# Three SSD products moved from GpSimd to VectorE, and one running account for the background work of a tick

## The chip, the cores and the metric

The kernel runs on one core of one Trainium2 chip. The metric is the device time of one execution in microseconds (us); lower is better. TensorE is called PE below, VectorE DVE, ScalarE ACT, GpSimd POOL, and SyncE, which issues the transfers, SP.

## The reference

One step of a one-layer hybrid decoder: 2048 prompt tokens and 8 sample sequences of 4 tokens share the weights. A wide projection feeds a convolution branch (value times sigmoid of a gate, a depthwise convolution of 31 taps) and a Mamba-2 branch, which are merged and projected.

```python
proj = h @ w_in
conv_val, conv_glu, conv_gate, z, xbc, dt_raw, m_conv, m_ssm = split_cols(proj, IN_SIZES)
u, new_conf_buf = causal_dwconv(conv_val * jax.nn.sigmoid(conv_glu), conf_buf, conf_dw_w, conf_dw_b)
...
xbc = jax.nn.silu(xbc)
xs, bm, cm = split_cols(xbc, ...)
# ssd_scan, in chunks of 128 tokens
decay = jnp.exp(jnp.where(mask, seg, -jnp.inf))
cb = jnp.einsum('bcqgn,bckgn->bcqkg', cc, bc)
y_intra = jnp.einsum('bcqkgr,bckgrp->bcqgrp', cb[..., None] * decay, xdt)
st = jnp.einsum('bcqgn,bcqgrp->bcgrpn', bc, xdt * decay_end[..., None])
y_inter = jnp.einsum('bcqgn,bcgrpn->bcqgrp', cc, h_starts) * jnp.exp(cum)[..., None]
...
y = y.reshape(bsz, L, SSM_DIM) * jax.nn.silu(z)
y = rmsnorm(y.reshape(bsz, L, SSM_GROUPS, SSM_DIM // SSM_GROUPS), 1.0).reshape(bsz, L, SSM_DIM) * ssm_norm_g
```

## The kernel before

There are two passes. Pass 1 (to about 2460 us) does the wide projection with the SSD scan inside it; pass 2 does the output projections. The change touches pass 1 alone.

**Ticks.** Pass 1 treats the tokens in two halves: half 0 has 1056 tokens in three token blocks of 352 columns, half 1 has 1024 in two blocks of 512. Within a half it goes through eight groups of heads; a group has ten blocks of weights (B, C, four of x, a merge block, the gates and values of the convolution, an even and an odd z). One block of weights times one token block is a tick: 24 matmuls in `mm3`, since each fp32 product is made of a high and a low part (`hh`, `hl` and `wh`, `wl`; L136 to L138). The result lies in a PSUM tile `acc` until `evac` reads it. The low part of each weight tile is made on DVE at L129, the high part on ACT at L128.

**SSD units.** A unit is one chunk of 128 tokens for one group of four heads. Half 0 has nine units in a group, half 1 eight, and a new one begins every three or two ticks. `prefetch` loads a tile `se` of 128x1024 from memory; ACT subtracts and clips it (L611, four times) and takes the exponential (L613). Its first half then holds factors by which C is scaled, its second half (`un["m"]`) the decay matrix. `ssd_a_pe` makes transposes and the product C times B on PE; `ssd_a_vec` makes out of them `cbm` (L654), the scaled x `xe` and `xd` (L661, L662), the high parts `bt` and `xh` on ACT, and the low parts `bl` (L671, DVE) and `xl` (L669, POOL). The scaling of C (L652) and the product of decay and `cbm` (L656) are on POOL, too. Some ticks later (four in half 0, three in half 1, two in group 7) `ssd_b_pe` uses all of it: PE L701 reads the product, L704 the scaled C, L710 to L712 the parts of x and B. `ssd_b_vec` adds up on DVE (L723 to L733).

**Gating.** After a z block ACT makes its silu (L775), DVE multiplies it onto the group's output (`set`, L806). After the odd block ACT squares (L813), DVE adds the two squares (`sp`, L814) and PE sums over the group (L825, `group_sums`), in the program two ticks later (`SUMS_AGE`); ACT takes that sum out of PSUM at L828. PE works in program order: where L814 is late, PE stands still at L825.

**Background work.** Three queues of generators fill DVE between these: `hi` (the four-tap convolution of x, B and C, L543), `mid`, and `lo` (the 30 taps of the other convolution, L574, each 128x1024). In each tick a budget is set (3300 in half 0, 5000 in half 1), the unit's costs are taken off (1450 and 1700), `hi` runs with what is left, and `lo` with what `hi` leaves, but with no less than 1200. Each tick starts with a new budget. A scheduler then orders the instructions of each engine by their priorities (`PRIO_*`); what it decides is shown below for the places at issue.

Of the kernel before, what the change touches and what calls it, by code (L numbers as in the profile page):

```python
# [7 lines left out]
F32 = mybir.dt.float32  # L8
# [17 lines left out]

PRIO_SPLIT, PRIO_EVAC, PRIO_MID, PRIO_SSD = 300, 300, 100, 100
GATE_AT = 5
SUMS_AGE = 2
T2 = 416  # L30
NT2 = NTOK // T2
# [9 lines left out]
for _n, _w in (("sw", 128), ("sb", 32), ("cw", 248), ("cb", 8), ("lng", 8), ("lnb", 8), ("dsk", 16),  # L41
               ("ng", 16), ("gpre", 8), ("gpost", 8), ("bada", 24), ("alog", 32), ("dtb", 1)):
    PRM[_n] = (_o, _w)
    _o += _w
NPRM = _o

CST = {}
_o = 0
# [37 lines left out]
class Kernel:  # L86
# [560 lines left out]
    def ssd_a_vec(self, un):  # L647
        V, S = self.V, self.S
        half, g, c, se, tr, w = (un[k] for k in ("half", "g", "c", "se", "tr", "w"))
        hs = slice(4 * g, 4 * g + 4)  # L650
        if c < 8 and not un["zero"]:
            self.G.tensor_tensor(out=se[:, 0:4], in0=se[:, 0:4], in1=bc(un["C"], "p (o q) -> p o q", [P, 4, P], o=1), op=ALU.mult)  # L652
        cbm = self.a1.tile([P, P], F32, tag="cbm", name="cbm", bufs=2)
        V.tensor_tensor(out=cbm[:w, :w], in0=tr[:w, 384:384 + w], in1=self.c_("tri") if c < 8 else self.c_("btri", NH)[:, :NH], op=ALU.mult)  # L654
        M = un["m"][:w, :, :w]
        self.G.tensor_tensor(out=M, in0=M, in1=bc(cbm[:w, :w], "p (o q) -> p o q", [w, 4, w], o=1), op=ALU.mult)  # L656
        xd = self.a1.tile([P, 4, 64], F32, tag="xd", name="xd", bufs=2)
        xe = self.a1.tile([P, 4, 64], F32, tag="xe", name="xe", bufs=1)
        w3 = w if c < 8 else 96
        xt = tr[:w3, 0:256].rearrange("p (h q) -> p h q", h=4)  # L660
        V.tensor_tensor(out=xe[:w3], in0=xt, in1=bc(self.dte[half][:w3, c, hs], "p (h o) -> p h o", [w3, 4, 64], o=1), op=ALU.mult)  # L661
        V.tensor_tensor(out=xd[:w], in0=xt[:w], in1=bc(self.dt[half][:w, c, hs], "p (h o) -> p h o", [w, 4, 64], o=1), op=ALU.mult)  # L662
        bt = self.a1.tile([P, P], F32R, tag="bt", name="bt", bufs=2)
        if c < 8:
            S.activation(out=bt, in_=tr[:, 256:384], func=AF.Copy)
            xh = un["xh"] = self.a1.tile([P, 4, 64], F32R, tag="xh", name="xh", bufs=2)
            S.activation(out=xh, in_=xe, func=AF.Copy)  # L667
            xl = un["xl"] = self.a1.tile([P, 4, 64], F32R, tag="xl", name="xl", bufs=2)
            self.G.tensor_tensor(out=xl, in0=xe, in1=xh.bitcast(F32), op=ALU.subtract)  # L669
            bl = un["bl"] = self.a1.tile([P, P], F32R, tag="bl", name="bl", bufs=2)  # L670
            V.tensor_tensor(out=bl, in0=tr[:, 256:384], in1=bt.bitcast(F32), op=ALU.subtract)  # L671
        else:
            S.activation(out=bt[:96], in_=tr[:96, 256:384], func=AF.Copy)
            V.tensor_tensor(out=bt[64:96], in0=tr[64:96, 256:384], in1=bt[64:96].bitcast(F32), op=ALU.subtract)
            xr = un["xr"] = self.a1.tile([P, 4, 64], F32R, tag="xr", name="xr")
            S.activation(out=xr[:96], in_=xe[:96], func=AF.Copy)
            V.tensor_tensor(out=xr[32:64], in0=xe[32:64], in1=xr[32:64].bitcast(F32), op=ALU.subtract)
            bm = self.se_tile().rearrange("p a q -> p (a q)").bitcast(F32R).rearrange("p (s n) -> p s n", s=NS)
            V.tensor_tensor(out=bm[:96], in0=bc(bt[:96].bitcast(F32), "p (o n) -> p o n", [96, NS, P], o=1),
                            in1=bc(self.c_("smask", 96), "p (s o) -> p s o", [96, NS, P], o=1), op=ALU.mult)  # L680
            un["bm"] = bm
        un["bt"], un["cbm"], un["xd"], un["xe"] = bt, cbm, xd, xe
# [74 lines left out]
    def evac(self, half, blk, tb, acc, env):  # L757
# [12 lines left out]
        elif kind in ("z", "gate", "m"):  # L770
            t = self.spp.tile([P, TB], F32, tag="sp", name="sp")
            if kind == "m":
                S.activation(out=t[:, :w], in_=acc[:, :w], func=AF.Tanh, scale=0.5)
            else:
                S.activation(out=t[:, :w], in_=acc[:, :w], func=AF.Silu)  # L775
            if kind == "z":
                self.gating(half, blk[1], off, w, t)
            else:
                Q.dma_start(self.D[kind][blk[1], :, gb:gb + w], t[:, :w])
        elif kind == "glu":  # L780
            t = self.spp.tile([P, TB], F32, tag="sp", name="sp")
            env.setdefault("tg", []).append(t)
            S.activation(out=t[:, :w], in_=acc[:, :w], func=AF.Tanh, scale=0.5)
        elif kind == "val":
            t = env["tg"][tb]
            u = env["u"]
            V.scalar_tensor_tensor(out=u[:, 30 + off:30 + off + npr], in0=t[:, :npr], scalar=1.0, in1=acc[:, :npr],
                                   op0=ALU.add, op1=ALU.mult)
            if npr < w:
                V.scalar_tensor_tensor(out=env["us"][:, :, 30:34], in0=t[:, npr:w].rearrange("p (s t) -> p s t", t=LS), scalar=1.0,  # L790
                                       in1=acc[:, npr:w].rearrange("p (s t) -> p s t", t=LS), op0=ALU.add, op1=ALU.mult)
        elif kind == "dt":
            dtT = env["dtT"]
            S.activation(out=dtT[:64, off:off + w], in_=acc[:64, :w], func=AF.Identity, bias=self.p_("dtb")[:64])
            if npr < w:
                for r in (1, 2):
                    S.activation(out=dtT[:64, HALF + 32 * r:HALF + 32 * r + 32], in_=dtT[:64, HALF:HALF + 32], func=AF.Copy)

    def gating(self, half, j, off, w, t):

# [91 lines left out]
    def pass1(self):  # L892
# [64 lines left out]
        def tick_vec():  # L957
            cost = 0
            for un in due("b"):
# [1 line left out]
                if un.get("last"):  # L961
                    self.group_done(un)
                late.remove(un)
                cost += 1450 if un["c"] < 8 else 6000
            if queue and state["phase"] == 0:
                un = queue[0]
                self.ssd_a_vec(un)
# [1 line left out]
                un["inter"] = state["now"] + 1 if un["c"] == 8 else None  # L969
                late.append(un)  # L970
                seg(1)
                cost += 1700
            return cost

        def tick_post():
# [5 lines left out]
                queue.pop(0)  # L981
                state["phase"] = 0

        bi, ready = 0, []
        for half in range(2):
            H = HALVES[half]
            env = {}
# [1 line left out]
            for gi, grp in enumerate(groups):  # L989
# [41 lines left out]
                for tb, (off, w) in enumerate(H["tbs"]):  # L1031
                    hh, hl = (h[:, :, off:off + w] for h in self.h)
                    for i, blk in enumerate(grp):
# [12 lines left out]
                        if tb == 0 and i == len(grp) - 1:  # L1046
                            self.fetch(bi + i + 1)
                            self.fetch(bi + i + 2)
                        if tb == (0 if len(grp) == 1 else nt - 1) and i == (0 if len(grp) == 1 else 1):
                            self.split(bi + len(grp))  # L1050
                        budget = 3300 if half == 0 else 5000
                        with tc.high_priority(offset=PRIO_SSD):
                            budget -= tick_vec()
                        with tc.high_priority(offset=PRIO_MID):
                            self.mid.run(4000 if half == 0 else 6000)
                        budget = self.hi.run(budget)
                        self.lo.run(max(budget, 1200))
                        tick_post()
                        self.tick += 1
                        self.group_sums(SUMS_AGE)  # L1060
# [366 lines left out]
```

## Time and profile before

| | before |
|---|---|
| median of 3 runs | 3224.7 us (3219.37 to 3224.92) |
| profiled execution | 3223.02 us, of which the span of the engines is 3221.2 us |
| busy, share of the span | PE 97%, DVE 72%, ACT 51%, POOL 22% |

All starts below are us from the start of the span. An engine works through its own queue in order, so an idle time ahead of an instruction, with the engine that ended it, tells what was late. A group's mean duration is over all of its instructions; where two engines disturb each other, single rows of the timeline tell more.

### The profile page before, as it was taken

The page shows a single profiled execution, that of the slowest core. Times are in us where ns is not written, and L with a number is a line of the kernel's source. Part 1 is how long each engine was busy: PE and PEld are TensorE (multiplying, and loading weights), DVE is VectorE, ACT ScalarE, POOL GpSimd, SP SyncE. Part 2 cuts the span into 40 slices and gives each one's busy share as a digit, 9 for nine tenths or more (in the row PEclk, how much of TensorE's full clock was granted, in tenths as well). Part 3 has the DMA queues.
Part 4 walks back from the last instruction along what each step waited for, and adds up shares of the span by engine and source line. Part 5 has one row for each costly group of instructions (what it writes and reads, how often), then busy time and mean ns, then how long its engine had stood idle before and what let it go on. Part 6 is the DMA issues. An engine that isn't in the chain of part 4 may idle for free.

```text
span 3221.2 us, 47618 instructions
## 1 busy us (share of the span) xinstructions
PE 3135.7 (97%) x18532; PEld 2818.9 (88%) x18532; DVE 2335.1 (72%) x3224; ACT 1656.9 (51%) x2649; POOL 704.6 (22%) x650
## 2 busy tenths in 40 slices
PE   7999999999999999999999999999999999999998
PEld 5998989999898989888778787777878999999997
DVE  5697886968787684557966868758676877778654
ACT  5665554545454453555556556455535444535332
POOL 0142422324242321034323333223320000000000
PEclk9999999999999999999999999999999999999999
DMA  6433233232323243222222222232227757676752
GB/s 231 135 92 104 78 89 94 80 101 75 104 79 95 84 125 127 78 66 80 73 87 84 63 86 79 94 104 70 86 94 222 246 190 250 198 247 203 234 165 87
DMA packets 235571, 392.99 MB, mean 122 GB/s; under 512 B 31569, under 2 KB 171281, under 8 KB 234321
## 3 DMA queue, kind: packets, MB, share of 16 engines
q1 hardware_dynamic: 235344, 389.94, 39.4%
q8 instruction: 146, 2.39, 0.3%
q14 instruction: 81, 0.66, 0.1%
HBM read 314.66 MB, written 75.22 MB: 121 GB/s over the span
## 4 chain that ended last, share of the span: by engine, by line
PE 83%; DVE 8%; DMA 5%; ACT 2%; issue 1%; POOL 0%; SPq 0%; ACTq 0%; DVEq 0%; POOLq 0%
PE acc L136 24%; PE acc L138 24%; PE acc L137 24%; DMA se<-d_cum 4%; DVE acc L574 3%; PE ys L701 2%; PE ys L704 1%; PE ys L710 1%; DVE wl L129 1%; PE tr L639 1%; DVE set L543 1%; PE tr L297 1%; PE tr L633 0%; ACT se L611 0%; PE ys L712 0%
## 5 line engine op out<-in xcount | busy, mean ns | idle before, releaser
L136 PE MATMUL acc<-hh,wh 128*128 128x352 f32 (+1 forms) x3520 | 1254.9, 357 | 0.0
L138 PE MATMUL acc<-hh,wl 128*128 128x352 f32 (+1 forms) x3520 | 1239.2, 352 | 0.0
L137 PE MATMUL acc<-hl,wh 128*128 128x352 f32 (+1 forms) x3520 | 1239.1, 352 | 0.0
L129 DVE TENSOR_TENSOR wl<-wr,wh 128x1024 fp32r<-128x1024 f32 x336 | 445.9, 1327 | 440.6 <-ACT wh L128 439.9
L136 PEld LDWEIGHTS acc<-hh,wh 128*128 128x128 f32 x3520 | 665.5, 189 | 64.0 <-issue 3.9
L138 PEld LDWEIGHTS acc<-hh,wl 128*128 128x128 f32 x3520 | 664.9, 189 | 62.7 <-issue 0.6
L137 PEld LDWEIGHTS acc<-hl,wh 128*128 128x128 f32 x3520 | 666.0, 189 | 58.0 <-issue 0.7
L574 DVE SCALAR_TENSOR_TENSOR acc<-u,cwh,acc 128x1024 f32<-128x1024 f32 x480 | 687.1, 1432 | 5.7 <-ACT acc L557 0.6
L128 ACT ACTIVATE wh<-wr 128x1024 fp32r<-128x1024 f32 x336 | 355.0, 1057 | 507.8 <-PE acc L137 459.4
L611 ACT ACTIVATE se<-se,cum 128x128 f32<-128x128 f32 x544 | 176.4, 386 | 464.2 <-DMA se<-d_cum 422.2
L652 POOL TENSOR_TENSOR se<-se,set 128x512 f32<-128x512 f32 x120 | 195.5, 1629 | 640.2 <-ACT se L613 630.8
L656 POOL TENSOR_TENSOR se<-se,cbm 128x512 f32<-128x512 f32 x136 | 213.9, 1573 | 338.2 <-DVE cbm L654 332.7
L543 DVE SCALAR_TENSOR_TENSOR set<-raw,prm,set 128x1080 f32<-128x1080 f32 (+1 forms) x192 | 270.9, 1411 | 10.0 <-ACT set L535 9.4
L138 PE MATMUL acc<-yh,wl 128*128 128x416 f32 x640 | 226.0, 353 | 0.4 <-DVE wl L129 0.4
L136 PE MATMUL acc<-yh,wh 128*128 128x416 f32 x640 | 226.2, 353 | 0.0
L137 PE MATMUL acc<-yl,wh 128*128 128x416 f32 x640 | 223.4, 349 | 0.0
L1313 POOL TENSOR_TENSOR oo<-oo,x 128x416 f32<-128x416 f32 x4 | 5.1, 1269 | 811.5 <-DVE oo L1312 811.0
L669 POOL TENSOR_TENSOR xl<-xe,xh 128x256 fp32r<-128x256 f32 x128 | 161.3, 1260 | 54.4 <-ACT xh L667 52.0
L613 ACT ACTIVATE se<-se 128x1024 f32<-128x1024 f32 (+1 forms) x136 | 135.2, 994 | 2.4 <-DMA se<-d_cum 0.4
L613 ACT ACT_TABLE_LOAD x105 | 134.7, 1283 | 1.9
L137 PEld LDWEIGHTS acc<-yl,wh 128*128 128x128 f32 x640 | 120.3, 188 | 2.9 <-issue 1.0
L136 PEld LDWEIGHTS acc<-yh,wh 128*128 128x128 f32 x640 | 120.2, 188 | 1.6 <-issue 1.0
(264 smaller groups left out, 4358.8 us busy)
## 6 DMA issues: line engine op xcount, KB each, us to landing
wr<-win SPq DMA_DIRECT2D x176, 512.0 KB
wr<-wso SPq DMA_DIRECT2D x80, 512.0 KB
se<-d_cum SPq DMA_DIRECT2D x128, 256.0 KB
wr<-wco SPq DMA_DIRECT2D x40, 512.0 KB
wr<-wo SPq DMA_DIRECT2D x40, 512.0 KB
yy<-d_y SPq DMA_DIRECT2D x40, 416.0 KB
tm<-d_m SPq DMA_DIRECT2D x80, 208.0 KB
d_m<-sp SPq DMA_DIRECT2D x48, 176.0 KB
```

The lines of the kernel that those rows point to most:

```text
L128: self.S.activation(out=hi[:, :cols], in_=raw[:, :cols], func=AF.Copy)
L129: self.V.tensor_tensor(out=lo[:, :cols], in0=raw[:, :cols], in1=hi[:, :cols].bitcast(F32), op=ALU.subtract)
L136: self.PE.matmul(out, whi[:, w], hhi(k), start=first and k == 0, stop=False)
L137: self.PE.matmul(out, whi[:, w], hlo(k), start=False, stop=False)
L138: self.PE.matmul(out, wlo[:, w], hhi(k), start=False, stop=last and k == KD - 1)
L543: V.scalar_tensor_tensor(out=acc, in0=raw[:, k:k + L], scalar=w[:, k:k + 1], in1=acc, op0=ALU.mult, op1=ALU.add)
L574: V.scalar_tensor_tensor(out=a, in0=u[:, k:k + HALF], scalar=w[:, k:k + 1], in1=a, op0=ALU.mult, op1=ALU.add)
L611: self.S.activation(out=se[:, m + h, :w], in_=se[:, h, :w], func=AF.Relu, bias=col)
L613: self.S.activation(out=se[:, a:b, :w], in_=se[:, a:b, :w], func=AF.Exp, scale=-1.0)
L652: self.G.tensor_tensor(out=se[:, 0:4], in0=se[:, 0:4], in1=bc(un["C"], "p (o q) -> p o q", [P, 4, P], o=1), op=ALU.mult)
L656: self.G.tensor_tensor(out=M, in0=M, in1=bc(cbm[:w, :w], "p (o q) -> p o q", [w, 4, w], o=1), op=ALU.mult)
L669: self.G.tensor_tensor(out=xl, in0=xe, in1=xh.bitcast(F32), op=ALU.subtract)
```

## The change

Three tensor products of a unit are issued on VectorE in place of GpSimd: the scaling of C, the decay product (which is now written behind `xd`) and the low part of x (now behind `bl`). In the tick, the budget that started anew is replaced by one account `spare`: 4400 in half 0 or 6200 in half 1 are paid in, the cost of the block's own evacuation, of a weight split and of the units (with higher prices for these) are taken off, `hi` and `lo` run with the sum, a debt is carried to the next tick, what is left over is dropped, and the floor of 1200 for `lo` is gone.

```diff
+TICK = (4400, 6200)
...
         if c < 8 and not un["zero"]:
-            self.G.tensor_tensor(out=se[:, 0:4], in0=se[:, 0:4], in1=bc(un["C"], "p (o q) -> p o q", [P, 4, P], o=1), op=ALU.mult)
+            V.tensor_tensor(out=se[:, 0:4], in0=se[:, 0:4], in1=bc(un["C"], "p (o q) -> p o q", [P, 4, P], o=1), op=ALU.mult)
         cbm = self.a1.tile([P, P], F32, tag="cbm", name="cbm", bufs=2)
...
-        M = un["m"][:w, :, :w]
-        self.G.tensor_tensor(out=M, in0=M, in1=bc(cbm[:w, :w], "p (o q) -> p o q", [w, 4, w], o=1), op=ALU.mult)
...
+        M = un["m"][:w, :, :w]
+        V.tensor_tensor(out=M, in0=M, in1=bc(cbm[:w, :w], "p (o q) -> p o q", [w, 4, w], o=1), op=ALU.mult)
...
-            self.G.tensor_tensor(out=xl, in0=xe, in1=xh.bitcast(F32), op=ALU.subtract)
             bl = un["bl"] = self.a1.tile([P, P], F32R, tag="bl", name="bl", bufs=2)
             V.tensor_tensor(out=bl, in0=tr[:, 256:384], in1=bt.bitcast(F32), op=ALU.subtract)
+            V.tensor_tensor(out=xl, in0=xe, in1=xh.bitcast(F32), op=ALU.subtract)
...
+    def evac_cost(self, half, blk, w):
+
+        if blk[0] == "z":
+            return (1 + blk[1] % 2) * (60 + w)
+        return 60 + w if blk[0] == "val" else 0
...
-                cost += 1450 if un["c"] < 8 else 6000
+                cost += 1500 if un["c"] < 8 else 6000
...
-                cost += 1700
+                cost += 2900 if un["c"] < 8 else 3200
...
+                        spare += TICK[half] - self.evac_cost(half, blk, w)
                         if tb == (0 if len(grp) == 1 else nt - 1) and i == (0 if len(grp) == 1 else 1):
                             self.split(bi + len(grp))
-                        budget = 3300 if half == 0 else 5000
+                            spare -= 1230
                         with tc.high_priority(offset=PRIO_SSD):
-                            budget -= tick_vec()
+                            spare -= tick_vec()
...
-                        budget = self.hi.run(budget)
-                        self.lo.run(max(budget, 1200))
+                        spare = min(self.lo.run(self.hi.run(spare)), 0)
```

In the changed kernel the line numbers are a little higher: the taps are L576, the weight split L131, the scaling of C L654, `cbm` L656, the decay product L664, `bl` L672, `xl` L673, the gating L814, the sum of squares L822, and on ACT the silu L777, the square L821, the clips L613 and the exponential L615.

**First place: DVE in the z blocks of group 1, half 0** (430 to 447 us before). Before, between the last two gating products of the group and the first sum of squares `sp`:

```order
L806 TENSOR_TENSOR set_1417<-set_1417,sp_4196 128x352
L654 TENSOR_TENSOR cbm_4237<-tr_4201,cst_71 128x128
L661 TENSOR_TENSOR xe_4241<-tr_4201,dte_422 128x256
L662 TENSOR_TENSOR xd_4240<-tr_4201,dt_421 128x256
L574 SCALAR_TENSOR_TENSOR acc_4120<-u_3760,cwh_428,acc_4120 128x1024 x3
L806 TENSOR_TENSOR set_1417<-set_1417,sp_4259 128x352
L671 TENSOR_TENSOR bl_4250<-tr_4201,bt_4244 128x128
L574 SCALAR_TENSOR_TENSOR acc_4120<-u_3760,cwh_428,acc_4120 128x1024
L814 TENSOR_TENSOR sp_4262<-sq2_4263 128x352
```

The same stretch of DVE's order now:

```order
L814 TENSOR_TENSOR set_1417<-set_1417,sp_4195 128x352
L656 TENSOR_TENSOR cbm_4236<-tr_4200,cst_71 128x128
L661 TENSOR_TENSOR xe_4239<-tr_4200,dte_422 128x256
L662 TENSOR_TENSOR xd_4238<-tr_4200,dt_421 128x256
L664 TENSOR_TENSOR se_4080<-se_4080,cbm_4236 128x512
L576 SCALAR_TENSOR_TENSOR acc_4120<-u_3760,cwh_428,acc_4120 128x1024
L654 TENSOR_TENSOR se_4198<-se_4198,set_2892 128x512
L576 SCALAR_TENSOR_TENSOR acc_4120<-u_3760,cwh_428,acc_4120 128x1024
L814 TENSOR_TENSOR set_1417<-set_1417,sp_4256 128x352
L672 TENSOR_TENSOR bl_4248<-tr_4200,bt_4243 128x128
L673 TENSOR_TENSOR xl_4247<-xe_4239,xh_4245 128x256
L576 SCALAR_TENSOR_TENSOR acc_4120<-u_3760,cwh_428,acc_4120 128x1024
L822 TENSOR_TENSOR sp_4259<-sq2_4260 128x352
```

Four taps have become three, and the decay product (L664), the scaling of C for a later unit (L654) and `xl` (L673) have come in. Groups 2 to 6 have the same order here.

**Second place: DVE in a unit of the following x blocks** (half 0, 505 to 516 us before). Now:

```order
L545 SCALAR_TENSOR_TENSOR set_4346<-raw_4641,prm_70,set_4346 128x1080
L576 SCALAR_TENSOR_TENSOR acc_4120<-u_3760,cwh_428,acc_4120 128x1024 x2
L654 TENSOR_TENSOR se_4925<-se_4925,set_2892 128x512
L576 SCALAR_TENSOR_TENSOR acc_4120<-u_3760,cwh_428,acc_4120 128x1024
L656 TENSOR_TENSOR cbm_4964<-tr_4927,cst_71 128x128
L661 TENSOR_TENSOR xe_4967<-tr_4927,dte_422 128x256
L662 TENSOR_TENSOR xd_4966<-tr_4927,dt_421 128x256
L664 TENSOR_TENSOR se_4644<-se_4644,cbm_4964 128x512
L131 TENSOR_TENSOR wl_5106<-wr_4957,wh_5105 128x1024
L672 TENSOR_TENSOR bl_4976<-tr_4927,bt_4971 128x128
L673 TENSOR_TENSOR xl_4975<-xe_4967,xh_4973 128x256
```

The scaling of C of a unit two further on (`se_4925`) now stands on DVE ahead of everything that the present unit (`se_4644`) needs. Before, POOL held it, and DVE had here only the rows that follow:

```order
L662 TENSOR_TENSOR xd_4970<-tr_4930,dt_421 128x256
L129 TENSOR_TENSOR wl_5107<-wr_4960,wh_5106 128x1024
L671 TENSOR_TENSOR bl_4980<-tr_4930,bt_4974 128x128
L543 SCALAR_TENSOR_TENSOR set_4350<-raw_4788,prm_70,set_4350 128x1080 x2
L725 TENSOR_TENSOR hT_417<-hd_5032,ys_4995 128x256
```

**Third place: DVE in the z blocks of group 0, half 0** (289 to 303 us before). Here the third gating product of the odd block stood behind three taps:

```order
L671 TENSOR_TENSOR bl_2799<-tr_2750,bt_2793 128x128
L564 TENSOR_TENSOR se_2610<-us_2267,cwh_428 128x4x31 x2
L574 SCALAR_TENSOR_TENSOR acc_2608<-u_2266,cwh_428,acc_2608 128x1024
L568 TENSOR_REDUCE acc_2608<-se_2610 128x16
L574 SCALAR_TENSOR_TENSOR acc_2608<-u_2266,cwh_428,acc_2608 128x1024
L571 TENSOR_SCALAR acc_2608<-acc_2608,prm_70 128x32
L574 SCALAR_TENSOR_TENSOR acc_2608<-u_2266,cwh_428,acc_2608 128x1024
L806 TENSOR_TENSOR set_437<-set_437,sp_2808 128x352
L574 SCALAR_TENSOR_TENSOR acc_2608<-u_2266,cwh_428,acc_2608 128x1024
L814 TENSOR_TENSOR sp_2811<-sq2_2812 128x352
```

Now:

```order
L673 TENSOR_TENSOR xl_2791<-xe_2783,xh_2789 128x256
L570 TENSOR_REDUCE acc_2663<-se_2665 128x16
L814 TENSOR_TENSOR set_437<-set_437,sp_2800 128x352
L566 TENSOR_TENSOR se_2665<-us_2267,cwh_428 128x4x31 x4
L576 SCALAR_TENSOR_TENSOR acc_2663<-u_2266,cwh_428,acc_2663 128x1024
L570 TENSOR_REDUCE acc_2663<-se_2665 128x16
L576 SCALAR_TENSOR_TENSOR acc_2663<-u_2266,cwh_428,acc_2663 128x1024
L822 TENSOR_TENSOR sp_2803<-sq2_2804 128x352
```

The gating product (`set_437`) has moved ahead of the taps, and two taps and the small product of L571 have moved behind the sum. On ACT, the square of that block (`sq2`, L813) stood behind two clips of the next unit's tile `se_2900`:

```order
L613 ACT_TABLE_LOAD
L613 ACTIVATE se_2748<-se_2748 128x1024
L775 ACT_TABLE_LOAD
L775 ACTIVATE sp_2808<-acc_2755 128x352
L611 ACTIVATE se_2900<-se_2900,cum_423 128x128 x2
L813 ACTIVATE sq2_2812<-set_437 128x704
```

Now:

```order
L777 ACTIVATE sp_2800<-acc_2749 128x352
L613 ACTIVATE se_2742<-se_2742,cum_423 128x128
L615 ACT_TABLE_LOAD
L615 ACTIVATE se_2742<-se_2742 128x1024
L821 ACTIVATE sq2_2804<-set_437 128x704
L777 ACT_TABLE_LOAD
L777 ACTIVATE sp_2836<-acc_2808 128x352
L613 ACTIVATE se_2893<-se_2893,cum_423 128x128 x4
```

The silu of the block (`sp`) stands ahead of the exponential, and its square ahead of every clip of the next unit's tile.

## Rows read from the trace of the kernel before

**Rows 1.** Windows, the two halves of pass 1: busy time, granted clock, DMA share, GB/s:

```profile
68.00:1330.00 1262.00, 1224.59 (x8405) 1169.23 (x8404) 951.37 (x1387) 662.28 (x1185) 362.99 (x367) 0.98 0.34 97
1330.00:2460.00 1130.00, 1118.46 (x5944) 889.57 (x5943) 807.89 (x1074) 624.12 (x957) 334.74 (x268) 1.00 0.28 86
```

**Rows 2.** Waits of PE: us in total, times, longest:

```profile
PE ys L825 <- DVE sp L814: 33.8, 8, 5.1
...
PE ys L307 <- ACT sp L828: 5.0, 1, 5.0
...
PE ys L825 <- ACT sp L828: 2.5, 1, 2.5
PE ys L712 <- DVE bl L671: 2.1, 2, 1.5
PE tr L690 <- POOL sp L885: 1.9, 1, 1.9
```

**Rows 3.** Timeline of DVE in group 1: start, duration, in brackets the idle time:

```profile
438.61 5.77 DVE L574 SCALAR_TENSOR_TENSOR acc<-u,cwh,acc 128x1024 f32<-128x1024 f32 x3
...
444.94 1.27 DVE L574 SCALAR_TENSOR_TENSOR acc<-u,cwh,acc 128x1024 f32<-128x1024 f32 x1
446.14 0.51 DVE L814 TENSOR_TENSOR sp<-sq 128x352 f32<-128x352 f32 x1
```

**Rows 4.** Timeline of POOL in the same stretch:

```profile
438.12 1.30 POOL L656 TENSOR_TENSOR se<-se,cbm 128x512 f32<-128x512 f32 x1 [5.01 <-DVE cbm L654]
439.82 1.82 POOL L652 TENSOR_TENSOR se<-se,set 128x512 f32<-128x512 f32 x1 [0.41 <-ACT se L613]
442.07 1.23 POOL L669 TENSOR_TENSOR xl<-xe,xh 128x256 fp32r<-128x256 f32 x1 [0.43 <-ACT xh L667]
```

**Rows 5.** Timeline of PE, group sums of groups 0 and 1:

```profile
302.63 0.52 PE L825 MATMUL ys<-sp,cst 128*32 128x88 f32 x8 [4.11 <-DVE sp L814]
```

```profile
446.70 0.52 PE L825 MATMUL ys<-sp,cst 128*32 128x88 f32 x8 [4.59 <-DVE sp L814]
```

**Rows 6.** Windows of PE behind its waits: PE busy, granted clock, DMA share, GB/s:

```profile
446.70:451.84 5.14, 5.14 (x26) 0.50 0.19 71
302.63:308.40 5.77, 5.77 (x28) 0.50 0.19 64
...
1165.07:1168.60 3.53, 3.53 (x25) 0.52 0.29 93
1556.84:1561.20 4.36, 4.36 (x20) 0.61 0.41 142
2074.98:2080.00 5.02, 5.02 (x28) 0.50 0.70 220
275.49:279.00 3.51, 3.51 (x32) 1.00 0.65 184
```

**Rows 7.** Groups of DVE and POOL instructions: busy, mean ns, idle before, releasers:

```profile
L574 DVE SCALAR_TENSOR_TENSOR acc<-u,cwh,acc 128x1024 f32<-128x1024 f32 x480 | 687.1, 1432 | 5.7 <-ACT acc L557 0.6
...
L662 DVE TENSOR_TENSOR xd<-tr,dt 128x256 f32<-128x256 f32 x128 | 52.9, 413 | 0.0
...
L747 DVE TENSOR_TENSOR acc<-acc,ys 128x512 f32<-128x512 f32 x32 | 21.3, 685 | 2.4 <-PE ys L742 2.0
```

```profile
L652 POOL TENSOR_TENSOR se<-se,set 128x512 f32<-128x512 f32 x120 | 195.5, 1629 | 640.2 <-ACT se L613 630.8 <-PE ys L712 4.8 <-PE acc L138 2.2
```

**Rows 8.** Timeline, z blocks of half 1 (DVE) and of group 0 (DVE, ACT):

```profile
1551.67 1.78 DVE L806 TENSOR_TENSOR set<-set,sp 128x512 f32<-128x512 f32 x1
```

```profile
301.95 0.53 DVE L814 TENSOR_TENSOR sp<-sq 128x352 f32<-128x352 f32 x1 [1.74 <-ACT sq L813]
```

```profile
300.55 0.69 ACT L611 ACTIVATE se<-se,cum 128x128 f32<-128x128 f32 x2 [4.06 <-DMA se<-d_cum]
```

**Rows 9.** Timelines of ACT and PE at the second place:

```profile
510.65 1.06 ACT L613 ACTIVATE se<-se 128x1024 f32<-128x1024 f32 x1
```

```profile
522.41 0.44 PE L701 MATMUL ys<-se,xd 128*64 128x128 f32 x4
```

More of the change, by code (lines that the diff above doesn't have):

```diff
@@ L982, in tick_post @@
                 state["phase"] = 0
-        bi, ready = 0, []
+        bi, ready, spare = 0, [], 0
         for half in range(2):
```

## The prediction

> **What bounds the kernel now.** The windows come first. In the two halves of pass 1 PE is busy for 1224.59 of 1262 us and 1118.46 of 1130 [rows 1], so PE sets the time, and a change to other engines can give or take what PE stands idle, 37.4 and 11.5 us, and what it runs slowly. DVE is busy for 951.37 us in half 0, 75%, and 71% in half 1; POOL for 29% and 30%.
>
> Next the waits of PE [rows 2]. Of the idle time, 33.8 us in 8 waits are group sums (L825) that wait for DVE's sum of squares (L814). Seven of them, one in the z blocks of each of the groups 0 to 6 in half 0, make 33.0 us; the eighth, 0.8, lies in half 1, where the group sums wait another 2.5 us and the gate's small matmuls (L307) 5.0 us for ACT's L828, which itself comes behind that sum. L712 waits 2.1 us for `bl`. Two of the seven are 4.11 us in group 0 and 4.59 in group 1 [rows 5].
>
> Then the clock behind the waits [rows 6]. After the wait of group 1 the granted clock is 0.50, the lower of the two levels (1.2 GHz), for 5.14 us, which at 2.4 GHz would have been 2.57 us of work: 2.57 us lost. After group 0 it is 2.9 us, after the seventh 1.7; the seven together 14.6 us, worked out in the same way. In half 1 it is 1.7 us behind the wait of 2.5 (0.61 for 4.36 us) and 2.5 us behind that of 5.0. Behind the wait of 1.9 us [rows 2] the clock stayed at 1.00 [rows 6]. So one wait of 4 to 5 us costs 6 to 7.
>
> Last, what DVE does ahead of such a sum. In group 1 three taps take 5.77 us, the one behind them 1.27 [rows 3], and the next instruction starts 1.20 after it. During the three, POOL works off the decay product, the scaling of C and `xl`, from 438.12 to 443.30 with two short pauses [rows 4]. Three taps alone would have taken 3.67 (1.27 and twice 1.20), so 2.1 us of the wait of 4.59 come from the two engines being in each other's way.
>
> The Trainium skill has a rule for it (SBUF — State Buffer, on who interferes with whom): a DVE instruction with two SBUF inputs and a GpSimd instruction that reads SBUF contend, and the second to issue is held until the first is done. The rows agree in direction, both engines being longer here; that one is held for the whole of the other they don't show.
>
> **The change part by part.** (1) *The moved products.* 120 scalings of C, 136 decay products and 128 `xl` leave POOL. On DVE none of these was seen; the nearest row is an fp32 product of 128x512, 685 ns, and one of 128x256, 413 ns [rows 7]. That makes 256 x 0.685 + 128 x 0.413 = 228 us more DVE work. In return, DVE's own work gets shorter where POOL was in its way: the 480 taps have a mean of 1432 ns against 1.27 alone [rows 3, 7], which gives 78 us at most, and the gating, the splits and the four-tap convolution add some more. I take +100 us over pass 1, between +70 and +228. None of it is on PE's path in itself. DVE was idle for 311 us in half 0 and 322 in half 1 [rows 1]; that is the cover.
>
> (2) *Groups 1 to 6, half 0 (first place).* Instructions overlap by about 0.07 us (a tap of 1.27 is followed after 1.20), so I charge 0.61 for 128x512 and 0.34 for 128x256. Ahead of the sum stand one tap less (-1.20), the decay product and a scaling of C (+1.22), and `xl` (+0.34): +0.36. The taps lose their 2.1. So the sum ends 1.74 us earlier, and a wait of 4.6 becomes 2.85. Does the scaling of C wait there? POOL got its exponential by 439.82 [rows 4]; DVE comes to it after `xd` (438.6), the product and one tap, at 440.4: no. Six groups: 6 x 1.74 = **10.4 us**. The clock behind a wait of 2.85 lies between those behind 1.9 and 4.6 [rows 6]; I take the loss of the wait of 2.5, 1.7 us, in place of a mean of 1.95: **1.5 us** in six.
>
> (3) *Group 0 (third place).* Here the sum started at 301.95 because ACT's square came late, and that stood behind clips that waited 4.06 us for a transfer of `se`, to 300.55 [rows 8]. The new order has the gating product ahead of the taps and the square ahead of all clips of that tile, so the transfer is out of it; what is ahead of the sum now are two taps, four small products and two reductions. PE reached L825 at 298.52 (302.63 less 4.11). The sum should be done by then: the whole wait and its clock go, 4.1 + 2.9 = **7.0 us**. If it isn't, some 3 us of this remain.
>
> (4) *Half 1.* At the wait of 2.5 us, DVE did a tap, a gating of 1.78 us [rows 8], a shape that takes 0.685 elsewhere [rows 7], and a split, in 5.0 us, all beside POOL. Now the decay product, the gating and the split stand there, 0.61 + 0.61 + some 1.2, and the gating must wait for its silu a few tenths: 2.1 us earlier, and 1.7 of clock if the rest of the wait, 0.4, leaves it up: **3.8**. At the wait of 5.0 the order is the same, but the split and the square wait for ACT: 1.7 us earlier and 0.5 of clock, **2.2**. The longest wait for `bl`, 1.5 [rows 2], was behind slowed taps: **1.5**.
>
> (5) *The account.* It lets fewer taps run in a tick of the z blocks, which is in (2) to (4), and more in others. It issues no instruction itself. Taps that are late are drained at the next value block, where DVE has nothing that PE waits for [rows 2]: nothing. If a drain of four taps stood ahead of a sum, it would cost 4 x 1.2 = 4.8 us there.
>
> (6) *The new wait.* POOL waited for the exponential ahead of almost every scaling of C, 630.8 us in all [rows 7]. On POOL that cost nothing; on DVE everything behind it waits too. At the second place the exponential ends at 511.71, and behind the scaling come 0.61, a tap 1.20, `cbm`, `xe` and `xd` 0.9, the decay product 0.61, a split 1.2, `bl` and `xl` 0.5: 5.0 us, so `xl` is there at 516.7, and PE wants this unit from 522.41 [rows 9]. The slack is 5.7 us. The transfers and the exponentials keep their order, so I charge nothing. The bound above: in group 7, where a unit has only two ticks, the slack is smaller, and 1 to 2 us there, in two or three units, would cost 5 us.
>
> Sum: 10.4 + 1.5 + 7.0 + 3.8 + 2.2 + 1.5 = 26.4 us. The profiled execution took 3223.0 us (median 3224.7, so the sum needs no correction that matters): 3223.0 - 26.4 = 3196.6, forecast **3197 us**.
>
> **The rivals.** *All waits go.* If DVE keeps ahead everywhere (POOL's disturbance was larger than single rows show, or fewer taps stand ahead), the rest of (2) goes too: 6 x 2.85 and the clock of 1.7 in six, 27 us more: 3170. With all idle time and slow clock of pass 1 gone it would be 48.9 + 18.8 = 68 us, 3155, the bound. For it speaks that a wait below 2 leaves the clock up; against it, that (2) counts instruction by instruction.
>
> *No relief.* The taps stay long (transfers or ACT lengthen them), and the moved products come on top: +0.36 in six groups, half 1 unchanged, group 0 gains: 3223 + 2 - 7 = 3218, within what a measurement can tell from no change (0.2%, 6.4 us). Against it: the tap of 1.27 right behind POOL's last instruction.
>
> *DVE and ACT in a ring: slower.* DVE waits for the exponential; behind it stands `xe`, for which ACT's `xh` waits, and ACT has the next clips and exponential behind `xh`. If that delays each exponential beyond the slack of 5.7 us, every unit of half 0, 72 of them, stops PE. From there each us costs 72 us with the clock to follow; at 1 us in two thirds of the units it takes 48 us, so 3245. For it: the 630.8 us. Against it: `xh` stands on ACT far ahead of the exponential that DVE waits for.
>
> *DVE becomes the bound.* With 100 us more, about half of them in half 0, DVE is at 79% there. Were the added work all to fall where DVE has no idle time, 3223 + 100 = 3323. The Trainium skill (Perfetto Trace Analysis, on optimizing Scalar and DVE operations) says that work of a saturated DVE may go to Scalar or GpSimd, which is against this change; it also says that the two share a port, so that moving between them may not help. Idle time of 311 us stands against it [rows 1].
>
> **How the numbers follow.** The forecast 0.58, all waits going 0.2, no relief 0.1, the ring 0.09, DVE the bound 0.03. The forecast's own range is 3187 to 3210: (3) failing is +4, (2) mis-sized by half is 5 to 10 either way. The range for 8 in 10 reaches down to 3168, with most of the second case, and up to 3214. Faster by over 0.2%: 0.78; within: 0.1; slower: 0.12.
>
> **What would show it.** POOL's busy time falls from 705 us to about 135. Single taps are 1.27 us throughout. L825 waits for L814 some 2.9 us in groups 1 to 6, not at all in group 0. DVE gets waits for the exponential ahead of the scaling of C, and none of them shows up at PE's L701. It is wrong if L701 or L711 waits for DVE, or if the waits at L825 stay above 4 us.

## The result, and the profile after

The changed kernel takes 3196.3 us in the median of 4 runs (3188.67 to 3202.86), before 3224.5; the ratio is 0.9917, 95% interval 0.9906 to 0.9929. The forecast was 3197 us. Five more runs gave 3198.2 (3189.58 to 3203.48), ratio 0.9915 (0.9902 to 0.9929). The time is as forecast, but not every term of the sum is; the profile shows which. Of the runs below one execution lies far outside, 17469.74 us of the kernel with the account alone, and no ratio counts it.

The page of the changed kernel, busy time, share and instructions of each engine:

```profile
PE 3119.7 (98%) x18532; PEld 2804.1 (88%) x18532; DVE 2360.9 (74%) x3608; ACT 1654.0 (52%) x2646; POOL 144.1 (5%) x266
```

The two halves of pass 1 in windows, as [rows 1]:

```profile
68.00:1330.00 1262.00, 1237.13 (x8520) 1176.97 (x8519) 976.30 (x1617) 685.38 (x1206) 89.76 (x179) 1.00 0.35 98
1330.00:2460.00 1130.00, 1125.42 (x5999) 900.29 (x5999) 836.79 (x1271) 618.35 (x962) 47.92 (x72) 1.00 0.31 93
```

POOL has gone from 705 to 144 us, and DVE's total has grown from 2335.1 us by 26 us only. The granted clock of half 0 is 1.00 now, 0.98 before.

The groups of DVE, as [rows 7]:

```profile
L576 DVE SCALAR_TENSOR_TENSOR acc<-u,cwh,acc 128x1024 f32<-128x1024 f32 x480 | 615.3, 1282 | 4.0
L131 DVE TENSOR_TENSOR wl<-wr,wh 128x1024 fp32r<-128x1024 f32 x336 | 411.9, 1226 | 238.4 <-ACT wh L130 237.4
...
L664 DVE TENSOR_TENSOR se<-se,cbm 128x512 f32<-128x512 f32 x128 | 87.4, 683 | 0.0
L654 DVE TENSOR_TENSOR se<-se,set 128x512 f32<-128x512 f32 x120 | 82.7, 689 | 114.3 <-ACT se L615 114.3
...
L673 DVE TENSOR_TENSOR xl<-xe,xh 128x256 fp32r<-128x256 f32 x128 | 53.3, 416 | 3.2 <-ACT xh L669 3.2
```

Each moved product costs what the nearest row said (0.685 and 0.413 us), and the three add 223 us. The taps have a mean of 1282 ns in place of 1432. The scaling of C does wait for the exponential, 114.3 us in all.

The waits of PE, as [rows 2]:

```profile
PE ys L833 <- DVE sp L822: 19.5, 8, 3.4
...
PE ys L703 <- ACT sp L836: 2.7, 1, 2.7
PE ys L309 <- ACT sp L836: 2.4, 1, 2.4
PE ys L315 <- ACT sp L331: 2.0, 1, 2.0
```

33.8 us at the group sums have become 19.5, all of it in half 0; the waits for `bl` (L672) are gone, as are the 0.8 and 2.5 us of half 1. No wait for the scaling of C is in the list, and for `xl` one of 0.2 us (it isn't shown here).

DVE in the z blocks of group 1, as [rows 3]:

```profile
435.03 1.28 DVE L576 SCALAR_TENSOR_TENSOR acc<-u,cwh,acc 128x1024 f32<-128x1024 f32 x1
436.23 0.68 DVE L654 TENSOR_TENSOR se<-se,set 128x512 f32<-128x512 f32 x1
436.83 1.28 DVE L576 SCALAR_TENSOR_TENSOR acc<-u,cwh,acc 128x1024 f32<-128x1024 f32 x1
438.03 0.52 DVE L814 TENSOR_TENSOR set<-set,sp 128x352 f32<-128x352 f32 x1
...
439.00 1.28 DVE L576 SCALAR_TENSOR_TENSOR acc<-u,cwh,acc 128x1024 f32<-128x1024 f32 x1
440.19 0.52 DVE L822 TENSOR_TENSOR sp<-sq 128x352 f32<-128x352 f32 x1
```

PE at the group sums of groups 0 and 1, as [rows 5]:

```profile
300.37 0.36 PE L833 MATMUL ys<-sp,cst 128*32 128x88 f32 x8 [0.99 <-DVE sp L822]
...
440.76 0.36 PE L833 MATMUL ys<-sp,cst 128*32 128x88 f32 x8 [2.68 <-DVE sp L822]
```

And the clock behind the waits of groups 1 and 2, windows as [rows 6], here with all engines' busy time:

```profile
440.76:446.00 5.24, 5.24 (x47) 4.76 (x49) 5.24 (x8) 2.39 (x5) 0.00 (x0) 1.00 0.18 69
580.99:586.00 5.01, 5.01 (x45) 4.64 (x45) 5.01 (x8) 2.22 (x4) 0.00 (x0) 1.00 0.22 76
```

Single taps are 1.28 us, the wait is 2.68, and PE runs at full clock right behind it: 47 matmuls in 5.24 us, where 26 fitted into 5.14 before. The other four windows show 1.00, too. The group sums start 5.9 us earlier than before in group 1 (440.76 against 446.70) and 24.0 us earlier in group 6 (1141.07 against 1165.07).

### The profile page after: what moved, and what is told of

The parts are those of the page before. It is cut to its first block, busy times and chain, and to the rows that moved or that the text cites. A ratio compares the mean times of both kernels' runs of the same rounds, so it can differ in the third digit from the quotient of the medians.

```text
span 3186.9 us, 47318 instructions
## 1 busy us (share of the span) xinstructions
PE 3119.7 (98%) x18532; PEld 2804.1 (88%) x18532; DVE 2360.9 (74%) x3608; ACT 1654.0 (52%) x2646; POOL 144.1 (5%) x266
## 4 chain that ended last, share of the span: by engine, by line
PE 86%; DMA 5%; DVE 5%; ACT 2%; issue 1%; SPq 0%; ACTq 0%; DVEq 0%
PE acc L138 25%; PE acc L140 25%; PE acc L139 25%; DMA se<-d_cum 4%; PE ys L703 3%; PE ys L706 2%; PE ys L712 1%; DVE acc L576 1%; PE tr L641 1%; PE tr L635 0%; PE ys L713 0%; PE ys L714 0%; DMA d_hx<-set 0%; DMA X<-xT 0%; PE tr L637 0%
## 5 line engine op out<-in xcount | busy, mean ns | idle before, releaser
L576 DVE SCALAR_TENSOR_TENSOR acc<-u,cwh,acc 128x1024 f32<-128x1024 f32 x480 | 615.3, 1282 | 4.0
L131 DVE TENSOR_TENSOR wl<-wr,wh 128x1024 fp32r<-128x1024 f32 x336 | 411.9, 1226 | 238.4 <-ACT wh L130 237.4
L613 ACT ACTIVATE se<-se,cum 128x128 f32<-128x128 f32 x544 | 175.0, 387 | 488.4 <-DMA se<-d_cum 471.6
L545 DVE SCALAR_TENSOR_TENSOR set<-raw,prm,set 128x1080 f32<-128x1080 f32 (+1 forms) x192 | 251.6, 1310 | 1.3 <-ACT set L537 1.1
L654 DVE TENSOR_TENSOR se<-se,set 128x512 f32<-128x512 f32 x120 | 82.7, 689 | 114.3 <-ACT se L615 114.3
L615 ACT ACTIVATE se<-se 128x1024 f32<-128x1024 f32 (+1 forms) x136 | 135.3, 995 | 2.3
L140 PEld LDWEIGHTS acc<-yh,wl 128*128 128x128 f32 x640 | 120.0, 187 | 0.9
L703 PE MATMUL ys<-se,xd 128*64 128x128 f32 x1088 | 114.0, 282 | 2.7 <-ACT sp L836 2.7
L138 PE MATMUL acc<-mh,wh 128*128 128x416 f32 x320 | 114.1, 357 | 0.0
```

Of the source, the lines that this page charges most:

```text
L131: self.V.tensor_tensor(out=lo[:, :cols], in0=raw[:, :cols], in1=hi[:, :cols].bitcast(F32), op=ALU.subtract)
L138: self.PE.matmul(out, whi[:, w], hhi(k), start=first and k == 0, stop=False)
L140: self.PE.matmul(out, wlo[:, w], hhi(k), start=False, stop=last and k == KD - 1)
L545: V.scalar_tensor_tensor(out=acc, in0=raw[:, k:k + L], scalar=w[:, k:k + 1], in1=acc, op0=ALU.mult, op1=ALU.add)
L576: V.scalar_tensor_tensor(out=a, in0=u[:, k:k + HALF], scalar=w[:, k:k + 1], in1=a, op0=ALU.mult, op1=ALU.add)
L613: self.S.activation(out=se[:, m + h, :w], in_=se[:, h, :w], func=AF.Relu, bias=col)
```

## The experiments

**The account or the move?** Two kernels with one part each. The first is the kernel before with the new account, the second the changed kernel with the old budget:

```diff
# account_only, against before
+                        spare += TICK[half] - self.evac_cost(half, blk, w)
-                        budget = 3300 if half == 0 else 5000
...
-                        self.lo.run(max(budget, 1200))
+                        spare = min(self.lo.run(self.hi.run(spare)), 0)
# move_only, against the changed kernel
-                        spare += TICK[half] - self.evac_cost(half, blk, w)
+                        budget = 3300 if half == 0 else 5000
...
-                        spare = min(self.lo.run(self.hi.run(spare)), 0)
+                        budget = self.hi.run(budget)
+                        self.lo.run(max(budget, 1200))
```

> The account alone, the three products still on GpSimd. In group 1 DVE's order ahead of the sum of squares is that of before, four taps. Theory (GpSimd's reads lengthen DVE's instructions, so the move is what gains): taps keep a mean of about 1.43 us, the waits at the group sums of groups 1 to 6 stay 4.6 to 5.1 us with the low clock behind them, only group 0 and single places gain: 3212 to 3222 us. Rival (the account gains, by having fewer taps where PE waits): 3205 us or less.

> The three products on VectorE, the old budget of each tick. Theory: taps at 1.27 to 1.29 us, waits of groups 1 to 6 at 2.5 to 3.4 us, group 0 keeps its wait of about 4 us, since that was a matter of order: 3200 us, between 3195 and 3206. Rival (the account gains): 3215 us or more.

The account alone: 3224.2 us, ratio 0.9996 (0.9987 to 1.0006). The move alone: 3198.1 us, ratio 0.9907 (0.9893 to 0.9922), the changed kernel's own. So the whole gain is the move's. With the account alone the taps keep a mean of 1423 ns and PE waits as before. It does gain in group 0 (waits of 1.0 and 0.3 us, where 4.1 was), but the waits of groups 1 to 6 are a little longer (29.9 us in all, 28.9 before), and two short ones early in half 0 have grown or come in, 2.1 us at L495 (0.5 before) and 1.4 at L165:

```profile
PE ys L831 <- DVE sp L820: 32.3, 9, 5.4
...
PE ys L495 <- DVE acc L491: 2.2, 2, 2.1
```

With the move alone:

```profile
PE ys L833 <- DVE sp L822: 21.5, 8, 3.6
```

Its waits of groups 1 to 6 are 2.1 to 3.6 us, 18.1 in all. Group 0 has two of 1.7 us, 3.4 in all, where one of about 4 was expected. In each of groups 1 to 6 DVE's order from `xd` to the sum is the changed kernel's, with three taps, while the account alone has the four of before: the tap that has gone from there went with the move, not with the account.

**The contention put back.** The changed kernel, with GpSimd products of the old sizes beside each unit; they read `cbm` and write a tile that nobody uses, so DVE's order stays that of the changed kernel (in the traces, too, all 3608 of DVE's instructions come in the same order):

```diff
         V.tensor_tensor(out=M, in0=M, in1=bc(cbm[:w, :w], ...), op=ALU.mult)
+        dum = self.a1.tile([P, 4, P], F32, tag="dum", name="dum", bufs=1)
+        cb4 = bc(cbm[:w, :w], "p (o q) -> p o q", [w, 4, w], o=1)
+        for n in (4, 4, 2) if c < 8 else (4,):
+            self.G.tensor_tensor(out=dum[:w, :n, :w], in0=cb4[:, :n], in1=cb4[:, :n], op=ALU.mult)
```

> The changed kernel, and beside each unit three GpSimd products of the old sizes whose results nobody uses; DVE's order is that of the changed kernel. Theory (two engines at SBUF in each other's way): GpSimd is busy for some 560 us again, taps go back to a mean of 1.40 to 1.45 us, the waits of groups 1 to 6 to about 5 us with the low clock behind them; 3215 to 3235 us. Rival (the gain is one of order and of the account, not of contention): within 6 us of the changed kernel, 3190 to 3203.

3223.5 us, ratio to before 0.9995 (0.9986 to 1.0003): the whole gain is gone, though DVE still does all the work in the changed kernel's order. But the means are not those expected. Busy time, the groups of DVE and the wait of PE at the group sums in this run:

```profile
PE 3133.5 (97%) x18532; PEld 2815.7 (87%) x18532; DVE 2522.5 (78%) x3608; ACT 1653.4 (51%) x2646; POOL 633.1 (20%) x658
...
L576 DVE SCALAR_TENSOR_TENSOR acc<-u,cwh,acc 128x1024 f32<-128x1024 f32 x480 | 627.9, 1308 | 4.0
...
L664 DVE TENSOR_TENSOR se<-se,cbm 128x512 f32<-128x512 f32 x128 | 142.6, 1114 | 0.0
...
L677 DVE TENSOR_TENSOR xl<-xe,xh 128x256 fp32r<-128x256 f32 x128 | 91.3, 714 | 2.5 <-ACT xh L673 2.5
...
PE ys L837 <- DVE sp L826: 31.6, 10, 5.3
```

The taps are at 1308 ns, not 1400 to 1450; the decay product has gone from 683 to 1114 and `xl` from 416 to 714, since the dummies start with `cbm` and meet those first. DVE is busy for 2522.5 us, 162 more than without them, and GpSimd for 633.1, where 560 were expected. The waits of groups 1 to 6 are 3.9 to 5.3 us, 28.5 in all, against 17.9 without the dummies.

**Where it costs.** The same dummies, beside the units of the z blocks only, and beside all others only (the condition `self.cur == "z"` or its opposite, `self.cur` being the kind of the tick's block).

> The changed kernel with the unused GpSimd products beside those units only that are issued in a tick of a z block. Theory (the disturbance costs at the group sums): the waits of groups 1 to 6 are 4 to 5 us as with the dummies everywhere, low clock follows each: 3208 to 3222 us. Rival (it costs in every unit a little): 3203 us or less, since few of the units lie there.

> The counterpart: the unused GpSimd products beside all other units. Theory: VectorE gets slower there, too, but PE waits for nothing of it: waits of groups 1 to 6 near 3 us, 3194 to 3208 us. Rival (it costs in every unit): 3212 us or more.

In z blocks: 3211.1 us, ratio 0.9959 (0.9947 to 0.9971), as the theory had it. In all others: 3209.8, 0.9956 (0.9943 to 0.9969), between the theory and its rival. Against the changed kernel's 3197 that is 14 and 13 us, each give or take some 4, which together make up the 26 of the dummies everywhere. POOL is busy for 221 us in the one and 553 in the other, 77 and 409 more than without dummies, so in a z block the disturbance costs several times as much for each us that POOL works. DVE in the z blocks of group 1 with the dummies there, and POOL, whose three products are taken one by one:

```profile
432.87 1.09 DVE L664 TENSOR_TENSOR se<-se,cbm 128x512 f32<-128x512 f32 x1
433.89 2.06 DVE L576 SCALAR_TENSOR_TENSOR acc<-u,cwh,acc 128x1024 f32<-128x1024 f32 x1
435.87 1.10 DVE L654 TENSOR_TENSOR se<-se,set 128x512 f32<-128x512 f32 x1
436.89 1.27 DVE L576 SCALAR_TENSOR_TENSOR acc<-u,cwh,acc 128x1024 f32<-128x1024 f32 x1
```

```profile
432.38 1.04 POOL L668 TENSOR_TENSOR dum<-cbm 128x512 f32<-128x512 f32 x1 [6.17 <-DVE cbm L656]
433.50 1.37 POOL L668 TENSOR_TENSOR dum<-cbm 128x512 f32<-128x512 f32 x1
434.95 1.48 POOL L668 TENSOR_TENSOR dum<-cbm 128x256 f32<-128x256 f32 x1
```

While POOL runs (432.38 to 436.43) DVE's three instructions take 1.09, 2.06 and 1.10 us, where they took 0.68, 1.28 and 0.68 without the dummies; the tap behind them takes 1.27. Each of the three began while a GpSimd product was under way, and ended 0.54, 1.08 and 0.54 us after that product's end. PE's waits at the group sums, with the dummies in z blocks and with the dummies elsewhere:

```profile
PE ys L837 <- DVE sp L826: 29.6, 8, 5.3
```

```profile
PE ys L837 <- DVE sp L826: 22.6, 9, 3.6
```

In z blocks the waits of groups 1 to 6 sum to 27.9 us, against 17.9 without the dummies, and low clock follows each of them. With the dummies elsewhere they stay at 19.3, as expected, but the theory that PE waits for nothing there was wrong: in group 0 and its surroundings waits of 1.8 (transposes L635), 2.5 (L696) and 2.7 us (L496) appear, three of about 1.1 at group sums, and one of 1.6 for `xl` in group 7; and there is more low clock.

**The exponential on DVE's queue.** The changed kernel with the scaling of C alone back on GpSimd (`V.tensor_tensor(out=se[:, 0:4]...` becomes `self.G.tensor_tensor`).

> The changed kernel with the scaling of C alone back on GpSimd (120 of the 384 products). Theory (VectorE's wait for the exponential, 114.3 us in 38 waits in the profile after, lies in time that VectorE has to spare and costs nothing): the wait goes, some taps get longer beside GpSimd, 3194 to 3210 us, no gain. Rival (the wait for the exponential holds up what PE needs): 3190 us or less.

3201.0 us, ratio to before 0.9929 (0.9917 to 0.9941): no gain from taking DVE's wait of 114.3 us away. The run puts some contention back along with it, so it shows no net gain and not that the wait costs exactly nothing; the waits of groups 1 to 6 grow to 22.6 us in total:

```profile
PE ys L833 <- DVE sp L822: 22.6, 6, 4.2
```

**The sums a tick later.** `SUMS_AGE = 3` in place of 2, in the changed kernel and in the one before.

> The changed kernel with the group sums three ticks behind the gating in place of two. Theory (what is left in pass 1 is PE in program order at the group sums, 19.5 us in the profile, and a low clock behind them in some executions): these waits and the low clock behind them go, 3168 to 3178 us, and the runs lie closer together. Rival (the waits come back one tick later, or at the tiles that the sums hold longer): 3188 us or more.

> The kernel before with the group sums three ticks behind the gating in place of two; the three products stay on GpSimd. Theory (what GpSimd's disturbance costs is paid almost only at the group sums: 33.8 us of waits in the trace of before and some 15 us of low clock behind them): 3176 to 3190 us, about as fast as the changed kernel with the same edit. Rival (the disturbance costs elsewhere too, or the sums are more than a tick late): 3200 us or more.

In the changed kernel 3183.8 us, ratio to before 0.9872 (0.9858 to 0.9885), between the two expectations; in the kernel before 3231.0, ratio 1.0018 (1.0009 to 1.0027). PE's waits at the group sums for DVE's sum of squares are gone in the one and down to 1.4 us in the other, so the sums were less than a tick late. But other waits stand in their place. In the changed kernel:

```profile
PE ys L833 <- ACT sp L836: 4.9, 4, 2.8
PE ys L315 <- ACT sp L331: 4.8, 2, 2.8
...
PE ys L703 <- ACT sp L836: 2.8, 1, 2.8
```

In the kernel before with the same edit:

```profile
PE ys L825 <- ACT sp L828: 17.8, 6, 4.6
PE ys L701 <- POOL se L652: 13.7, 5, 7.3
...
PE ys L313 <- ACT sp L329: 5.4, 3, 4.2
```

There ACT's copy of a sum (L828) is queued behind squares that wait for DVE's gating. At one of them this gating product takes 1.61 us beside POOL's decay product, 0.52 alone. ACT there, and PE behind it:

```profile
453.33 0.79 ACT L813 ACTIVATE sq<-set 128x704 f32<-128x704 f32 x1 [2.47 <-DVE set L806]
...
454.83 0.24 ACT L828 ACTIVATE sp<-ys 128x88 f32<-128x88 f32 x1
```

```profile
455.13 0.52 PE L825 MATMUL ys<-sp,cst 128*32 128x88 f32 x8 [2.62 <-ACT sp L828]
```

The longest wait for POOL's scaling of C, 7.3 us, isn't contention by its rows. POOL waited for the exponential, and ACT's clips ahead of that waited for their transfer:

```profile
1557.24 1.48 POOL L652 TENSOR_TENSOR se<-se,set 128x512 f32<-128x512 f32 x1 [11.06 <-ACT se L613]
...
1553.46 1.28 ACT L611 ACTIVATE se<-se,cum 128x128 f32<-128x128 f32 x4 [4.72 <-DMA se<-d_cum]
```

So my theory that the waits at the sums were almost the whole price is wrong for the kernel before: with them gone from DVE, PE waits elsewhere, for copies that contention helps to make late and for a late transfer, and its idle time in the two halves of pass 1 doesn't shrink (51.7 us, 48.9 before). Why that transfer came later there is open.

**The copy of a sum.** With the sums later, the copy on VectorE (`self.V.tensor_copy`), or on ScalarE at a higher priority (`self.tc.high_priority(offset=500)` around it).

> The changed kernel with the group sums three ticks behind, and their copy out of PSUM on VectorE in place of ScalarE. Theory (the waits that were left, 2.8 us at a group sum of group 0 and 2.8 us in group 7, came from ScalarE's copy being queued behind clips that wait for a transfer; low clock followed one of them for 3.4 us): both go, 3171 to 3181 us. Rival (the copy waits as long in VectorE's queue): 3182 us or more.

> The changed kernel with the group sums three ticks behind and the copy of a sum on ScalarE, but at a higher priority, so that in most groups it stands ahead of a copy of the projection or of the clips that follow. Theory (the 10 us of waits for that copy, with those behind it and their clock, are ScalarE's order): 3174 to 3182 us. Rival (the copy was held by clips that still stand ahead of it, waiting for their transfer): 3182 to 3187 us, no change from the version without the priority.

On VectorE it takes 3189.1 us, ratio 0.9890 (0.9875 to 0.9905): the rival. The copy waits as long in DVE's queue (PE waits 13.7 us for it, at L703 and L833, against 7.7 with the copy on ACT). At higher priority: 3178.3 us, ratio to before 0.9855 (0.9843 to 0.9868), the lowest time here, in the expected range, though its interval overlaps that of the version without the priority. Yet its waits for the copy are 7.1 us against 7.7, so the reason expected isn't shown; between the two profiles (3184.8 and 3179.6 us) PE's busy time differs by 5.4 us at the same matmuls, which is clock, at least 3.4 of it in stretches that the windows show.

**A second profile of the changed kernel.**

> The changed kernel once more, for a second profile and more runs. Theory (whether the clock falls behind a wait of some 3 us differs from one execution to the next, and that alone spreads the runs from 3189 to 3203 us): this profile has the same waits, 2.5 to 3.5 us in groups 1 to 6, and its time differs from the first profile's 3188.7 us by the stretches of low clock, each some 1.7 or 3.4 us. Rival (the waits themselves differ): the waits of groups 1 to 6 sum to something else than 17.9 us by as much as the times differ.

Its time is 3189.6 us; the waits of groups 1 to 6 sum to 18.1 us, against 17.9 in the first profile. Windows of PE behind three of them (2.54, 3.08 and 3.54 us):

```profile
440.23:444.00 3.77, 3.77 (x23) 0.59 0.25 96
582.00:586.00 4.00, 3.99 (x33) 1.00 0.26 90
1142.57:1146.00 3.43, 3.42 (x28) 0.71 0.26 86
```

The clock fell behind two waits behind which it had stayed up in the first profile. Over all nine executions of the changed kernel, the mean granted clock goes with the time, with one exception: 0.995 and 0.994 at 3188.7 and 3189.6 us, 0.991 and 0.992 from 3195.8 to 3203.5, but 0.994 at 3197.5. A difference of 0.003 is some 9.6 us of 3190. So in the two profiles the waits repeat and the clock behind them doesn't. That clock makes up most of the spread is an estimate from these means; that it is all of it isn't shown. Both profiles fell on runs with little low clock, and the median is some 7.7 us above the first profile. In the second profile PE also waits for DVE in group 7, 0.7 us at L703 for the decay product and 0.6 at L713 for `xl`; DVE's queue runs without an idle time for 10 us ahead of both, so no wait for the exponential stands there.

## Why the prediction was right

The profile took 3188.7 us, 34.3 less than that of before; the sum had 26.4. The mechanism is the one forecast, but that the median lies within 1 us of the forecast is partly luck, as the terms show. Step by step:

*(1) The moved products.* 0.683, 0.689 and 0.416 us where 0.685 and 0.413 were taken: right. The net growth of DVE was sized at 100 us, lower bound 70, and is 26. Some 28 of the difference is overlap: the 228 counts whole durations, where step (2) charges 0.61 and 0.34 us, which would make 200. The rest is that contention had lengthened more than the taps (the splits went from 1327 to 1226 ns, the four-tap convolution from 1411 to 1310). This did no harm, as DVE isn't the bound.

*(2) Groups 1 to 6.* The waits went from 28.9 us to 17.9, 11.0 us, with 10.4 forecast; 2.98 in the mean where 2.85 was worked out. The mechanism is shown by the dummies: same DVE order, contention back, gain gone, and 10.6 us of these waits with it. The clock is where the size was off: I took 1.7 us as the loss behind each wait and 1.5 us gained in six, while the first profile lost nothing at all behind them, some 11.7 us gained. In the median run part of that is lost again.

*(3) Group 0.* Its wait was to go whole, 4.1 us; 1.7 remained (0.99 and 0.67), and its clock loss went. The failed step is "the transfer is out of it": the new order of ACT has the silu of the block behind three clips of the same unit's tile `se`, which my rows began just behind, and they wait for their transfer. DVE's gating waited 3.29 us for that silu, and the sum came behind it. The square of the token block after it stands behind four clips of the next unit's tile, which wait for a transfer, too; that is the 0.67:

```profile
294.13 0.99 ACT L613 ACTIVATE se<-se,cum 128x128 f32<-128x128 f32 x3 [3.27 <-DMA se<-d_cum]
295.02 0.44 ACT L777 ACTIVATE sp<-acc 128x352 f32<-128x352 f32 x1
295.50 0.53 DVE L814 TENSOR_TENSOR set<-set,sp 128x352 f32<-128x352 f32 x1 [3.29 <-ACT sp L777]
298.04 0.78 ACT L821 ACTIVATE sq<-set 128x704 f32<-128x704 f32 x1
...
303.30 1.28 ACT L613 ACTIVATE se<-se,cum 128x128 f32<-128x128 f32 x4 [2.71 <-DMA se<-d_cum]
304.48 0.78 ACT L821 ACTIVATE sq<-set 128x704 f32<-128x704 f32 x1
```

*(4) Half 1.* The waits of 0.8 and 2.5 us went with their clock, 5.0 us where 3.8 was said. The wait of 5.0 is 2.4 now, but the clock behind it is still 0.50 for 5 us (2041.03 to 2046.00), so 2.5 in place of 2.2. That for `bl` went: 1.5, as said.

*(5) The account* was costed at nothing, and is nothing in sum (0.9996). But it isn't what lets fewer taps run ahead of the sums of groups 1 to 6, as (5) says: the move alone has the same three. *(6) The new wait* is real, 38 times and 114.3 us, and no row of PE shows it; taking it away together with 120 of the products gains nothing. The ring between DVE and ACT didn't form, and DVE, busy for 74%, didn't become the bound.

Smaller waits that weren't in the sum came in and went out: 1.9 us at L690 gone, 2.7 at L703 and 2.0 at L315 new, both for ACT. With them the terms as measured make 34.2 us (11.0 + 11.7 + 5.3 + 5.0 + 2.5 + 1.5 - 2.8), what the profile gained. The clock gave 10.2 us more than the sum had, and group 0 and these waits 4.5 less. The median came out at the forecast because its runs, by their mean clock, lose some of what the profile doesn't; no row of the forecast could say how much, so this agreement is luck.

## What to carry to other kernels

Compare one instruction's duration beside another engine's work with its duration alone before counting what a move to a busier engine adds: here 384 products moved onto the engine at 72%, and its total grew by 26 us, not 228. What contention costs is best tested by putting it back as useless work; in the kernel before, taking away the wait that shows it (the sums a tick later) only moved it, while the changed kernel gained 13 us by the same edit. And when reading a new order, read on ahead on each engine to the last instruction that waits for a transfer, not only to the one that moved.

## What the runs showed of the hardware

The clock behind a wait of PE of 2.5 to 3.6 us isn't settled by its length. Behind waits of 4.1 to 5.4 us in half 0 the granted clock fell in every profile here; behind 2.5 to 3.6 us it fell in some cases and not in others, in the same place of the same program (0.59 and 1.00 behind 2.54 and 2.68 us in group 1). Nor does a wait below 2 us always leave it up, as the prediction's second case took it from one row: behind 1.90 us it stayed at 1.00 in the kernel before [rows 6], but behind 1.67 us at L713 with the account alone it was 0.60 (2343.78 to 2348.00). In the kernel before, a fall behind a group sum cost 1.7 to 2.9 us of PE's time.

A DVE instruction that reads both its tensors from SBUF and begins beside a GpSimd product was held until that product ended. With the dummies everywhere, 33 taps and 127 decay products began while a GpSimd product was under way. None of them ended before it: all 33 taps ended 1.08 us behind its end, and all decay products 0.55 us, to 0.01 us. Alone they take 1.28 and 0.68. In the kernel before, 119 taps that began at least 0.25 us ahead of such an end came out 1.08 to 1.09 us behind it. `xd`, which reads x out of PSUM, isn't held: 126 of these products began beside a dummy and took 0.40 to 0.42 us, as alone. The Trainium skill says (SBUF — State Buffer, on who interferes with whom) that a DVE instruction with two SBUF inputs and a GpSimd instruction that reads SBUF contend for a port pair that is locked for one of them. These rows agree, and they settle what the prediction left open, whether one is held for the whole of the other.
